# Weight sums of the second MLP: two sets kept in HBM against one, with the other grown in SBUF by adding transfers

## The chip, the cores and the metric

One core of a Trainium2 chip. The metric is the device time of one execution in microseconds; the time of a kernel is the median of several runs, and a lower one is better. A profile is taken of one further execution, and its times are counted from the first instruction of that execution.

## The reference, cut to what matters

A two-layer decoder trunk on 512 tokens of 1024 channels, all in float32. Layer 0 mixes tokens with a Mamba-2 SSD, layer 1 with HGRN2. After each mixer comes a layer norm, a squared-ReLU MLP, a second layer norm and a gate:

```
for i in range(2):
    mix = ssd_mixer(x, ...) if i == 0 else hgrn2_mixer(x, ...)
    h = layer_norm(ALPHA * x + mix)
    h = layer_norm(ALPHA * h + (relu(h @ w1[i]) ** 2) @ w2[i])     # w1: 1024 x 4096, w2: 4096 x 1024
    x = h + sigmoid(h @ w_gate[i]) * (p[i] @ w_proj[i])
```

"MLP 1" below is that of layer 0 and "MLP 2" that of layer 1.

## The kernel before, in words

**Three products for one.** Every float32 matrix product is made of three matmuls on a rounded high part and a low part of each operand (`mm3`, lines 121 to 123). A weight tile of 128 x 1024 values (512 KB) arrives by a DMA that the SyncE queue (SP) issues into a ring of three buffers called `raw` (`unit`, line 107). ScalarE (ACT) then rounds it into `whi` (line 114) and VectorE (DVE) subtracts to get `wlo` (line 117); there are six buffers of each. `split` does the same two steps for a tile that is already in SBUF. "The 512 KB unit" below means one such tile.

**Seven block products for eight.** Both MLPs replace a product of 2 x 2 blocks by seven products of sums of blocks, as Strassen and Winograd do. For that, sums of weight blocks are needed (t1 to t4 for w2; for w1 the four sums of `pair`) and sums of activation blocks (`half_blocks`: s1 to s4). The seven products are p1 (a11 with w00), p2 (a12 with w10), p6 (s2 with t2), p7 (s3 with t3), p5 (s1 with t1), p4 (a22 with t4), p3 (s4 with w11). Each is 24 matmuls of 512 columns and uses two weight units.

**The order within an MLP.** The 4096 hidden channels are worked in four groups. `hidden(g)` makes the activations of group g in steps "T"; `block_product` multiplies group g-1 with w2 in steps "Q" (or two "q"). `PERIODS` (MLP 1) and `PAIRS` (MLP 2) write out the order: period 0 has only T, periods 1 to 3 mix both, and period 4 is seven products back to back, with the layer norm of the first two token chunks (`after(0), after(1)`) before its last two products.

**The sums of w2 in MLP 1** are made by `weight_sums`: eight loads per group on the GpSimd (POOL) queue into `r` tiles (line 382), then DVE additions (lines 389 to 397), then `split`.

**The sums for MLP 2** are made in advance. `block_sums` is a generator of 64 steps; each step is one or two DMAs on the POOL queue that copy or add blocks from HBM to HBM (line 270): into `s1` for w1 and into `s2` for w2. `add_blocks` takes the next steps and makes each DMA depend on a recent instruction (`paced`). It is called after every Q of the periods 1 to 3 of MLP 1 (one step in period 1, two in 2 and 3: 7 + 14 + 14 = 35 steps), then during HGRN2 after two of three yields of `hcore` (the other 29). In MLP 2 `pair` loads the sums of w1 with `unit(both(..))`, and `block_product` gets `stored`, so that t1 to t4 are loaded from `s2` with `unit` as any weight. In the profile both tensors have the name `s`, all loads of MLP weights `in_w`.

**Other places with tiles held together.** `gate` code of layer 0 (`mlp_and_gate`, after the periods) holds one unit of `wp` and four of `wg` at a time, for each half of the output columns. `out_project` with a norm behind it holds four units, and the next MLP's first three tiles follow it. `last_gate` loads its own block sums into `tb` tiles on POOL (lines 461 to 468).

**Tile scheduler.** Apart from TensorE in some stages, the order on each engine is set at build time by priorities: `tc.high_priority(offset=...)` moves instructions ahead (`LEAD` 100, `SOON` 40, `SUMS` up to 300). Each engine's queue is then executed in that order.

Of the kernel before, what the change touches and what calls it, by code (L numbers as in the profile page):

```python
# [8 lines left out]
F32 = mybir.dt.float32  # L9
# [6 lines left out]
P = 128  # L16
# [29 lines left out]
def trunk(ctx: ExitStack, tc, a):  # L46
# [4 lines left out]
    whip = pool("whip", 6)  # L51
    wlop = pool("wlop", 6)
    b8 = pool("b8", 9)
# [22 lines left out]
    mlp = dict(r=8, blk=2, sg=2)  # L76
    bufs = dict(ssd=dict(two, xs=4, sz=4, y=2, xdt=2, ecs=2, ss=2), mlp0=mlp, hgrn=dict(two, xs=4, sz=4, cv=4, y=2, pv=2, btok=2, sc=2, scb=2, qd=2), mlp1=dict(tb=4, blk=2, sg=2))
    phase = []
# [46 lines left out]
    class Split:  # L125
# [9 lines left out]
        def l(self, k, sl=slice(0, T)):  # L135
            return self.lo[k // 4][:, k % 4, sl]

    def project(src, xs, ps, m=P, tok=slice(0, T)):
# [94 lines left out]
    def block_sums():  # L233

        w1, w2, s1, s2 = (a[n] for n in ("w1_1", "w2_1", "s1", "s2"))
        rows = lambda v: v.rearrange("u p n -> (u p) n")
        wv = w1.rearrange("(q i) p (h n) -> i h q p n", i=2, h=2)
        sv = s1.rearrange("q p s n -> s q p n")
        for g in range(4):
            wa, wb, wc, wd = (rows(w2[8 * g + 2 * i : 8 * g + 2 * i + 2]) for i in range(4))  # L240
            t1, t2, t3, t4 = (rows(s2[8 * g + 2 * i : 8 * g + 2 * i + 2]) for i in range(4))
# [33 lines left out]
    def transpose_split(src, dst, c, apart, keep=None, whole=None):  # L275

        sl = slice(c * P, (c + 1) * P)
        for q in range(2):
            pt = bank(psm, "pm") if (c == 3 if keep is not None else apart and q) else bank(pst, "pt")
            for j in range(4):  # L280
                k = 4 * q + j
                nc.tensor.transpose(pt[:, j * P : (j + 1) * P], src[:, k * P : (k + 1) * P], ident)
            v = pt.rearrange("p (j t) -> p j t", j=4)
            h = dst.hi[q][:, :, sl]
            with tc.high_priority(offset=LEAD if apart or keep is not None else SOON):
                nc.scalar.copy(h, v)
                turned_last[:] = [nc.vector.tensor_sub(dst.lo[q][:, :, sl], v, f32(h))]
# [43 lines left out]
    def norm(i, keep=None, whole=None):  # L331

        gb = ln_params(i)
        h_s = Split(8)
        sums = mk(sm, [P, NCH, 2], "lnsum") if i else None
# [10 lines left out]
    def half_blocks(blk, z0, z1, p, plus):  # L346
# [52 lines left out]

    def block_product(w, blk, lead, first, after=None, turns=None, sums=None, low=None, stored=None):  # L400

        if stored is None:
            t1, t2, t3, t4 = weight_sums(w, lead, after=low)
        else:
            t1, t2, t3, t4 = stored
        seen = set() if first else {(i, j) for i in range(2) for j in range(2)}
        banks = {}

        def product(x, f, name, start, i, j, turns=None):
            made = stored is None and any(f is t for t in (t1, t2, t3, t4))  # L410
            us = [split(v) if made else unit(v) for v in f]
            if start:
                banks[name] = [bank(psy, "py%d" % c) if name == "x" else bank(psj, "pj") for c in range(2)]
            t = blk[x]
            for c in range(2):
# [10 lines left out]
                with tc.high_priority(offset=SOON if after else 0):  # L426
                    minus = stored is not None and j == 1
                    if after and x in ("a12", "s1", "a22", "s4"):
# [19 lines left out]
        p3 = lambda: product("s4", w[1][1], "x", False, 0, 1, turns)  # L448
        for f in (p1, p7, p6, p4, p5, p2, p3) if after else (p1, p2, p6, p7, p5, p4, p3):
            yield from f()  # L450
            if after and f is p5:
                after(0), after(1)
# [4 lines left out]
    def last_gate(wp, wg, h_s, p_s, kept, turned):  # L457
# [12 lines left out]
        pairs = [mk(b8, [P, 2, 4, 256], "b8", F32R) for _ in range(2)]  # L470
        cells = [mk(b8, [P, 4, T], "b8") for _ in range(3)] + [tmp("blk", [P, 4, T])]
        cell = lambda n: cells[n // 4][:, n % 4, :]
        tok = lambda c: slice(c * P, (c + 1) * P)
# [35 lines left out]
        def final(c, h, g, pp, pin=None):  # L509
            sg = tmp("sg", [P, T])  # L510
            with behind(pin):
# [164 lines left out]
    def mlp_and_gate(layer, h_s, last, whole=None):  # L676
# [5 lines left out]
        def hidden(g):  # L682
            names = ("a11", "a12", "a22", "s1", "s2", "s3", "s4")
            blocks[g] = {
                n: tmp("blk", [P, 2, 4, 256], F32R) if n in ("s3", "s4") else mk(b8, [P, 2, 4, 256], "b8", F32R)
                for n in names
            }
            for p in range(2):
# [17 lines left out]
                for r in range(2):  # L706
                    z = mk(w4, [P, 2, T], "ab"[r])
                    for i in range(2):
# [15 lines left out]
        for g, period in enumerate(PAIRS if whole is not None else PERIODS):  # L724
            if g < 4:
                tiles = hidden(g)
            if g > 0:
                if g == 4:
# [8 lines left out]
                w = [[[w2[8 * g - 8 + 4 * i + 2 * j + u] for u in range(2)] for j in range(2)] for i in range(2)]  # L737
                stored = [[a["s2"][8 * g - 8 + 2 * i + u] for u in range(2)] for i in range(4)] if whole is not None else None
                products = block_product(
                    w, blocks.pop(g - 1), SUMS[g - 1], g == 1, *((after, turned(0), sums) if g == 4 else ()), low=low if g == 1 else None, stored=stored  # L740
                )
# [720 lines left out]
    with tc.manual_schedule(engines={mybir.EngineType.PE}):  # L1462
        for h in range(0, 8, 2):
# [141 lines left out]
```

## Time and profile before

| what | value |
|---|---|
| median of 3 runs | 1451.97 us (1451.65 to 1452.2) |
| the profiled execution's own time | 1448.33 us |
| its span, first to last instruction | 1446.6 us |
| TensorE (PE) busy | 1412.2 us (98%), granted clock 0.992 |
| DVE / ACT / POOL busy | 1082.4 / 806.1 / 104.7 us |
| moved by DMA queue q1 (issued by SP) | 166.24 MB |
| moved by DMA queue q0 (issued by POOL) | 88.09 MB |

The stages follow one another: SSD until about 372 us, MLP 1 and its gate until about 800, HGRN2 until about 1050, MLP 2 until about 1370, the last gate until the end. PE is the busiest engine by far, so a microsecond counts where PE waits, or where its matmuls run at a lower granted clock; the idle time of the others counts only through that. A DMA "lands" when its data are complete; the time from issue to landing is what a consumer sees. "DMA share" is the mean busy share of the 16 DMA engines.

### The profile page before, as it was taken

What the parts mean: (1) busy time and instruction counts of PE and PEld (TensorE: products, weight loads), DVE (VectorE), ACT (ScalarE), POOL (GpSimd) and SP (SyncE); (2) the same over time, 40 slices, a digit from 0 to 9 for tenths busy, and PEclk for the clock granted to TensorE, in tenths of its full rate; (3) what the DMA queues carried; (4) which work ended last, traced back from release to release, by engine and by line L of the source; (5) the groups of instructions that cost most, each with busy time, mean ns of one, the idle gap of its engine ahead of it and who ended that gap; (6) DMA issues with size and microseconds to landing.
All of it is one profiled execution on the core that took longest, in us unless ns stands there. A gap on an engine that the chain in (4) does not pass through costs nothing.

```text
span 1446.6 us, 21844 instructions
## 1 busy us (share of the span) xinstructions
PE 1412.2 (98%) x8505; PEld 1189.2 (82%) x8505; DVE 1082.4 (75%) x1824; ACT 806.1 (56%) x1252; POOL 104.7 (7%) x148
## 2 busy tenths in 40 slices
PE   9999999999999999998899999999999999999898
PEld 7888888888988888786677888888799988888677
DVE  7989587788967657657767756777788776866795
ACT  6766465562453543544354656665577556664573
POOL 0000000001002011121200002122100000000000
PEclk9999999999999999998999999999999999999999
DMA  8434333235336678999961337988875656568731
GB/s 304 143 105 137 96 104 115 87 113 194 103 102 186 193 207 278 230 280 251 277 235 63 100 104 169 237 244 223 209 220 190 188 169 198 167 194 243 245 110 58
DMA packets 68904, 255.72 MB, mean 177 GB/s; under 512 B 7489, under 2 KB 8257, under 8 KB 66369
## 3 DMA queue, kind: packets, MB, share of 16 engines
q1 hardware_dynamic: 47424, 166.24, 34.2%
q0 software_dynamic: 21376, 88.09, 24.3%
q8 instruction: 67, 1.10, 0.3%
q14 instruction: 37, 0.30, 0.1%
HBM read 251.09 MB, written 65.08 MB: 219 GB/s over the span
## 4 chain that ended last, share of the span: by engine, by line
PE 41%; DVE 5%; DMA 5%; ACT 2%; issue 1%; ACTq 0%; DVEq 0%; SPq 0%
PE pj L121 9%; PE pj L122 9%; PE pj L123 9%; PE py L121 2%; PE py L122 2%; PE py L123 2%; DVE wlo L117 2%; DMA raw<-s 2%; DMA raw<-in_w 1%; ACT whi L114 1%; DMA raw<-in_wg 1%; PE py L1310 1%; PE pt L121 1%; PE pm L121 1%; DMA raw<-in_wp 1%
## 5 line engine op out<-in xcount | busy, mean ns | idle before, releaser
L117 DVE TENSOR_TENSOR wlo<-raw,whi 128x1024 fp32r<-128x1024 f32 (+1 forms) x278 | 330.5, 1194 | 195.4 <-ACT whi L114 194.1
L114 ACT CAST whi<-raw 128x1024 fp32r<-128x1024 f32 (+1 forms) x278 | 285.2, 1028 | 319.6 <-PE pj L122 149.4
L121 PE MATMUL pj<-b,whi 128*128 128x512 f32 (+1 forms) x878 | 323.3, 369 | 3.1 <-DVE b L668 2.4
L122 PE MATMUL pj<-b,whi 128*128 128x512 f32 (+1 forms) x878 | 321.4, 366 | 0.0
L123 PE MATMUL pj<-b,wlo 128*128 128x512 f32 (+1 forms) x878 | 321.0, 366 | 0.0
L123 PE MATMUL pj<-whi,b 128*128 128x512 f32 x520 | 204.1, 393 | 0.0
L121 PE MATMUL pj<-whi,b 128*128 128x512 f32 x508 | 202.1, 398 | 0.0
L122 PE MATMUL pj<-wlo,b 128*128 128x512 f32 x508 | 199.6, 393 | 0.0
L121 PEld LDWEIGHTS pj<-b,whi 128*128 128x128 f32 x878 | 165.5, 189 | 29.9 <-DVE b L668 2.8
L122 PEld LDWEIGHTS pj<-b,whi 128*128 128x128 f32 x878 | 165.9, 189 | 26.5 <-issue 0.9
L123 PEld LDWEIGHTS pj<-b,wlo 128*128 128x128 f32 x878 | 165.7, 189 | 25.8
L123 PEld LDWEIGHTS pj<-whi,b 128*128 128x128 f32 x520 | 98.0, 188 | 20.2
L121 PEld LDWEIGHTS pj<-whi,b 128*128 128x128 f32 x508 | 95.5, 188 | 19.3 <-ACT b L1457 0.3
L122 PEld LDWEIGHTS pj<-wlo,b 128*128 128x128 f32 x508 | 95.5, 188 | 18.4 <-issue 0.2
L121 PE MATMUL py<-whi,b 128*128 128x512 f32 x248 | 98.7, 399 | 9.1 <-DVE acc L435 7.0
L123 PE MATMUL py<-whi,b 128*128 128x512 f32 x260 | 102.5, 395 | 0.0
L122 PE MATMUL py<-wlo,b 128*128 128x512 f32 x248 | 98.1, 396 | 1.3 <-DVE wlo L117 1.3
L270 POOL DMA_DIRECT2D s<-in_w x66 | 61.1, 986 | 335.9 <-issue 149.0
L114 ACT CAST whi<-r 128x1024 fp32r<-128x1024 f32 x40 | 41.6, 1051 | 43.7 <-PE pj L123 18.4
L121 PEld LDWEIGHTS py<-whi,b 128*128 128x128 f32 x248 | 47.4, 191 | 20.8 <-DVE acc L435 9.1
L117 DVE TENSOR_TENSOR wlo<-r,whi 128x1024 fp32r<-128x1024 f32 x40 | 48.1, 1217 | 14.2 <-ACT whi L114 14.2
L123 PEld LDWEIGHTS py<-whi,b 128*128 128x128 f32 x260 | 49.5, 190 | 10.4
(437 smaller groups left out, 2416.6 us busy)
## 6 DMA issues: line engine op xcount, KB each, us to landing
raw<-in_w SPq DMA_DIRECT2D x98, 512.0 KB, 4.4
raw<-s SPq DMA_DIRECT2D x60, 512.0 KB, 4.1
s<-in_w POOLq DMA_DIRECT2D x42, 512.0 KB, 7.6
raw<-in_wssd SPq DMA_DIRECT2D x36, 512.0 KB, 3.9
r<-in_w POOLq DMA_DIRECT2D x32, 512.0 KB, 8.8
s<-in_w POOLq DMA_DIRECT2D x16, 1024.0 KB, 11.9
a<-csd SPq DMA_DIRECT2D x16, 512.0 KB, 3.7
raw<-in_wso SPq DMA_DIRECT2D x16, 512.0 KB, 3.3
```

The lines of the kernel that those rows point to most:

```text
L114: nc.scalar.copy(hi[:, :n], f)
L117: nc.vector.tensor_sub(lo[:, :n], f, f32(hi[:, :n]))
L121: nc.tensor.matmul(out, sh, mh, start=start, stop=False, **kw)
L122: nc.tensor.matmul(out, sh, ml, start=False, stop=False, **kw)
L123: return nc.tensor.matmul(out, sl, mh, start=False, stop=stop, **kw)
L270: dma = nc.gpsimd.dma_start(out, src, **(dict(accum_op=ALU.add, max_dma_last_dim=8192) if add else {}))
L1310: nc.tensor.matmul(pcs[r][bs, at : at + n], kk[r][:, ts], qs, start=True, stop=True)
```

## The change

The sums of w2 for MLP 2 are no longer made in HBM: the tensor `s2` and its 32 steps go, and `block_sums` keeps the 32 steps for w1. After a Q of MLP 1 one step is taken, in the periods 1 and 2 only (14 steps); in HGRN2 one is taken after every second yield (24 places for the other 18).

In MLP 2 `block_product` gets `grown`. Two pairs of `r` tiles are filled on the POOL queue: t3 = w11 and then + w01; t1 = w01 and then + w00. When t3 has been split for p7, w00 is added to the same tiles, which makes t2; when that has been split for p6, w10 is added, which makes t4. Each is a DMA with an add into SBUF. The order of the products becomes p1, p2, p7, p6, p4, p5, p3 (last group: p1, p7, p6, p5, p4, p2, p3).

Buffers: `wlo` has five buffers, not six; the `r` ring of this stage has four; the activation block s3 moves to the pool `b8`; the input of MLP 2 is held in four `b8` tiles cut by token halves (`Blocks`); the fourth of the first four tiles is projected in two halves of 256 tokens; the last gate's `sg` and one spare tile come from the `r` ring.

```diff
-    wlop = pool("wlop", 6)
+    wlop = pool("wlop", 5)
...
-    bufs = dict(..., mlp1=dict(tb=4, blk=2, sg=2))
+    bufs = dict(..., mlp1=dict(tb=4, r=4))
...
+    class Blocks:
+        def __init__(self):
+            self.t = [[mk(b8, [P, 2, 4, 256], "b8", F32R) for _ in range(2)] for _ in range(2)]
...
     def block_sums():        # the eight steps per group that write s2 are removed
-            yield [(t1, wb, False)]
             yield small(o2, b11, True)
-            yield [(t3, wb, False)]
             yield small(o4, o2, False)
-            yield [(t1, wa, True)]
             yield small(o4, b12, True)
-            yield [(t3, wd, True)]
-            yield [(t2, t3, False)]
-            yield [(t2, wa, True)]
-            yield [(t4, t2, False)]
-            yield [(t4, wc, True)]
...
-        put("s2", a11)
-        put("s3", a21)
+        put("s3" if plus else "s2", a21 if plus else a11)
+        put("s2" if plus else "s3", a11 if plus else a21)
...
-    def block_product(w, blk, lead, first, after=None, turns=None, sums=None, low=None, stored=None):
-        if stored is None:
+    def block_product(w, blk, lead, first, after=None, turns=None, sums=None, low=None, grown=False):
+        if grown:
+            t2, t1 = ([tmp("r", [P, 1024]) for _ in range(2)] for _ in range(2))
+            t3 = t4 = t2
+            def add_to(t, v, start=False):
+                for u in range(2):
+                    nc.gpsimd.dma_start(t[u], v[u], **({} if start else dict(accum_op=ALU.add)))
+            with tc.high_priority(offset=lead):
+                add_to(t3, w[1][1], True)
+                add_to(t1, w[0][1], True)
+                add_to(t3, w[0][1])
+                add_to(t1, w[0][0])
+            grow = {"s3": w[0][0], "s2": w[1][0]}
+        else:
             t1, t2, t3, t4 = weight_sums(w, lead, after=low)
-        else:
-            t1, t2, t3, t4 = stored
+            grow = {}
...
         def product(x, f, name, start, i, j, turns=None):
-            made = stored is None and any(f is t for t in (t1, t2, t3, t4))
-            us = [split(v) if made else unit(v) for v in f]
+            us = [split(v) if any(f is t for t in (t1, t2, t3, t4)) else unit(v) for v in f]
+            if x in grow:
+                with tc.high_priority(offset=LEAD):
+                    add_to(t2, grow[x])
...
+        if grown:
+            order = (p1, p7, p6, p5, p4, p2, p3) if after else (p1, p2, p7, p6, p4, p5, p3)
...
-        cells = [mk(b8, [P, 4, T], "b8") for _ in range(3)] + [tmp("blk", [P, 4, T])]
+        cells = [mk(b8, [P, 4, T], "b8") for _ in range(3)]
+        spare = tmp("r", [P, T])
...
-                            project(unit(w1[tiles[2 * r + i]], after=low if g == 0 and r == 0 else None), h_s, ps)
+                            u = unit(w1[tiles[2 * r + i]], after=low if g == 0 and r == 0 else None)
+                            for tok in [slice(0, T)] if whole is None else [slice(0, 256), slice(256, T)]:
+                                project(u, h_s, ps, tok=tok)
...
-                if op == "Q" and not last and g < 4:
-                    add_blocks(2 if g > 1 else 1)
+                if op == "Q" and not last and g in (1, 2):
+                    add_blocks()
...
-                if at % 3:
+                if at % 2:
                     add_blocks()
...
-    args["s2"] = nc.dram_tensor("s2", (32, P, D), F32).ap()
```

More of the change, by code (lines that the diff above doesn't have):

```diff
@@ L233, in block_sums @@
     def block_sums():
-        w1, w2, s1, s2 = (a[n] for n in ("w1_1", "w2_1", "s1", "s2"))
-        rows = lambda v: v.rearrange("u p n -> (u p) n")
+        w1, s1 = a["w1_1"], a["s1"]
         wv = w1.rearrange("(q i) p (h n) -> i h q p n", i=2, h=2)
@@ L426, in product @@
                 with tc.high_priority(offset=SOON if after else 0):
-                    minus = stored is not None and j == 1
+                    minus = grown and j == 1
                     if after and x in ("a12", "s1", "a22", "s4"):
@@ L448, in block_product @@
         p3 = lambda: product("s4", w[1][1], "x", False, 0, 1, turns)
-        for f in (p1, p7, p6, p4, p5, p2, p3) if after else (p1, p2, p6, p7, p5, p4, p3):
+        if grown:
+            order = (p1, p7, p6, p5, p4, p2, p3) if after else (p1, p2, p7, p6, p4, p5, p3)
+        else:
+            order = (p1, p7, p6, p4, p5, p2, p3) if after else (p1, p2, p6, p7, p5, p4, p3)
+        for f in order:
             yield from f()
-            if after and f is p5:
+            if after and f is order[4]:
                 after(0), after(1)
@@ L684, in hidden @@
             blocks[g] = {
-                n: tmp("blk", [P, 2, 4, 256], F32R) if n in ("s3", "s4") else mk(b8, [P, 2, 4, 256], "b8", F32R)
+                n: tmp("blk", [P, 2, 4, 256], F32R) if n == "s4" or n == "s3" and whole is None else mk(b8, [P, 2, 4, 256], "b8", F32R)
                 for n in names
@@ L737, in mlp_and_gate @@
                 w = [[[w2[8 * g - 8 + 4 * i + 2 * j + u] for u in range(2)] for j in range(2)] for i in range(2)]
-                stored = [[a["s2"][8 * g - 8 + 2 * i + u] for u in range(2)] for i in range(4)] if whole is not None else None
                 products = block_product(
-                    w, blocks.pop(g - 1), SUMS[g - 1], g == 1, *((after, turned(0), sums) if g == 4 else ()), low=low if g == 1 else None, stored=stored
+                    w, blocks.pop(g - 1), SUMS[g - 1], g == 1, *((after, turned(0), sums) if g == 4 else ()), low=low if g == 1 else None, grown=whole is not None
                 )
```

25 lines of the change are left out of this document (17 added, 8 removed).

## The prediction

> **What bounds the kernel now.** I read the cores' view first, then busy time by stage (columns: window, its length, then PE, PEld, DVE, ACT, POOL busy with their counts, the granted clock, the DMA share and GB/s).
>
> ```profile
> core 0: 1446.6 us, clock 0.992
> 372.00:592.00 220.00, 220.00 (x1039) 184.96 (x1039) 153.39 (x179) 104.49 (x135) 25.72 (x37) 1.00 0.63 189
> 592.00:730.00 138.00, 122.28 (x512) 98.49 (x511) 95.05 (x126) 62.31 (x85) 30.37 (x42) 0.94 0.95 262
> 785.00:800.00 15.00, 11.75 (x49) 9.13 (x48) 11.35 (x14) 5.99 (x11) 0.00 (x0) 0.89 0.17 55
> 850.00:1010.00 160.00, 160.00 (x1761) 131.51 (x1760) 118.78 (x377) 96.06 (x222) 27.75 (x33) 1.00 0.79 205
> 1010.00:1065.00 55.00, 53.28 (x405) 44.90 (x404) 42.53 (x87) 33.85 (x87) 7.51 (x10) 1.00 0.89 231
> 1065.00:1320.00 255.00, 254.37 (x1667) 231.95 (x1666) 195.32 (x255) 166.56 (x248) 1.34 (x2) 1.00 0.58 184
> 1320.00:1362.00 42.00, 35.55 (x161) 28.24 (x160) 27.68 (x35) 18.31 (x23) 5.25 (x8) 0.96 0.87 252
> ```
>
> PE is full wherever the DMA share is up to 0.79, and loses time in three places with a share of 0.87 or more: 138.00 - 122.28 = 15.72 us at the end of MLP 1, 42.00 - 35.55 = 6.45 us at the end of MLP 2, 1.72 us at the end of HGRN2. Only these, and 3.25 us in the gate at 785, can be won. The timeline of PE names the first place's waits, in brackets:
>
> ```profile
> 594.44 0.50 PE L121 MATMUL py<-whi,b 128*128 128x512 f32 x1 [1.40 <-DVE acc L435]
> 668.29 0.80 PE L121 MATMUL py<-whi,b 128*128 128x512 f32 x1 [2.82 <-DVE acc L435]
> 675.79 1.22 PE L121 MATMUL pj<-whi,blk 128*128 128x512 f32 x2 [2.99 <-ACT whi L114]
> 686.31 0.50 PE L122 MATMUL py<-wlo,b 128*128 128x512 f32 x1 [1.28 <-DVE wlo L117]
> 718.88 1.11 PE L282 MATMUL pt<-cst,acc 128*128 128x128 f32 x4 [5.95 <-DVE acc L225]
> 728.47 0.66 PE L282 MATMUL pt<-cst,acc 128*128 128x128 f32 x4 [1.18 <-DVE b L287]
> ...
> 597.32 0.39 PE L121 MATMUL pj<-b,whi 128*128 128x512 f32 x1
> 597.54 0.39 PE L122 MATMUL pj<-b,whi 128*128 128x512 f32 x1
> ...
> 668.89 0.63 PE L122 MATMUL py<-wlo,b 128*128 128x512 f32 x1
> 669.32 0.63 PE L123 MATMUL py<-whi,b 128*128 128x512 f32 x1
> ...
> 721.50 0.63 PE L123 MATMUL pj<-whi,b 128*128 128x512 f32 x1
> 721.93 0.63 PE L121 MATMUL pj<-whi,a 128*128 128x512 f32 x1
> ```
>
> Matmuls normally start 0.227 us apart; after the three long waits they start 0.43 us apart, 6 + 9 + 6 = 21 of them from 668.89 to 721.93: the clock was halved. That is another 21 x 0.2 = 4.2 us.
>
> The releasers are DVE and ACT, but what do these wait for? The ACT timeline, the chain of waits, the DMA views of two windows (a quiet one, 400 to 460, then 592 to 730; last column: us to landing), and POOL's timeline:
>
> ```profile
> 706.45 1.05 ACT L114 CAST whi<-raw 128x1024 fp32r<-128x1024 f32 x1 [5.56 <-DMA raw<-in_wp]
> 715.79 9.63 DMA raw<-in_wp
> ...
> raw<-in_w SPq DMA_DIRECT2D x8, 512.0 KB, 3.3
> r<-in_w POOLq DMA_DIRECT2D x6, 512.0 KB, 3.7
> ...
> q0 software_dynamic: 5841, 24.13, 69.0%
> s<-in_w POOLq DMA_DIRECT2D x13, 512.0 KB, 8.1
> raw<-in_w SPq DMA_DIRECT2D x12, 512.0 KB, 7.2
> r<-in_w POOLq DMA_DIRECT2D x8, 512.0 KB, 12.5
> raw<-in_wg SPq DMA_DIRECT2D x7, 512.0 KB, 9.6
> 722.72 0.87 POOL L270 DMA_DIRECT2D s<-in_w  x1 [7.52 <-DMA s<-s]
> ```
>
> POOL's queue fills 69% of the DMA engines, mostly with the sums for MLP 2, whose last transfer here leaves at 722.72. Beside it a 512 KB load takes 7 to 10 us, not 3.3. With three `raw` buffers and ACT and DVE in fixed order, the late load holds up everything behind its cast: layer norm and evictions included.
>
> **The change, part by part.**
>
> *Fewer steps in MLP 1.* Of 35 steps 14 stay, all in periods 1 and 2. One step lands in about 8.1 us, 14 x 8.1 = 113 us; two periods of 8 T and 7 Q last 2 x 15 x 24 x 0.227 = 163 us. So nothing is left over for period 3 and the seven products behind it: after about 590 only MLP 1's own loads run, as in 400 to 460. Waits that I take as gone: the two on `acc` (1.40 and 2.82; ACT was late with a cast before the burst of `half_blocks`), both layer norm waits (5.95 and 1.18; the loads of 706.45 and 715.79 stand ahead of them). With them 12 slow matmuls: 1.40 + 2.82 + 5.95 + 1.18 + 12 x 0.2 = 13.7 us. I leave standing the 2.99 and 1.28, since DVE makes the last group's sums only after p1's eviction, an order that fast loads need not mend. Bounds: all 15.72 + 4.2 = 19.9 gone, or only the two layer norm waits and six slow matmuls, 8.3.
>
> *HGRN2.* 18 steps for 29, and over before the last norm. PE is full in 850 to 1010, so nothing is gained there; of the 1.72 us after it I take half, -0.8 (0 to -1.7). The gate's 3.25 us at 785 have a DMA share of 0.17, so no load causes them: 0 (up to -3.25 if DVE's order changes).
>
> *Sums grown in MLP 2.* Per group, SP loads lose 8 units (stored sums); POOL gains 12 transfers, 4 starts and 8 adds. ACT and DVE do the same casts and subtractions. The rows of the end of MLP 2 (chain, DMA view of 1320 to 1362, POOL's timeline, groups; behind a queue stand its packets, MB and share):
>
> ```profile
> 1335.65 6.22 DMA raw<-s
> 1346.57 6.59 DMA raw<-s
> q1 hardware_dynamic: 1757, 6.39, 44.4%
> q0 software_dynamic: 1144, 4.18, 42.6%
> tb<-in_wg POOLq DMA_DIRECT2D x6, 512.0 KB, 6.7
> 1356.22 0.86 POOL L468 DMA_DIRECT2D tb<-in_wg  x1 [7.74 <-DMA tb<-tb]
> ...
> L117 DVE TENSOR_TENSOR wlo<-raw,whi 128x1024 fp32r<-128x1024 f32 (+1 forms) x278 | 330.5, 1194 | 195.4 <-ACT whi L114 194.1
> L114 ACT CAST whi<-raw 128x1024 fp32r<-128x1024 f32 (+1 forms) x278 | 285.2, 1028 | 319.6 <-PE pj L122 149.4
> ...
> 1050.88 0.28 PE L121 MATMUL pj<-b,whi 128*128 128x256 f32 x1
> 1051.00 0.28 PE L122 MATMUL pj<-b,whi 128*128 128x256 f32 x1
> ```
>
> Now the last seven products need 14 units in 7 x 5.45 us through three buffers, each held for 6.2 + 1.0 + 1.2 = 8.4 us: too slow. After the change 8 of the 14 bypass `raw`, so most of the 6.45 us goes; I count 5. In its place comes a chain: t3 split, add issued (0.86), landed (6.7), cast (1.03), subtracted (1.19) = 9.8 us, with p7 (5.45 us) to cover it. If the split ends when p7 starts, PE waits 4.35 us; if one product earlier, nothing. I take 3, since tiles for two products fit in five `wlo` buffers only just. From p6 to p4 there are two products (10.9 us), so nothing, unless POOL stands behind a `tb` wait (7.74 us, as above), which would cost 9.8 + 7.74 - 10.9 = 6.6. Sum -2, bounds -6.45 and +11. In the middle groups T steps lie between the products: a T is about 28 matmuls of 0.12 us = 3.4 us, so p7's start to p6's start is 5.45 + 2 x 3.4 = 12.2 us: hidden at a landing of 6.7.
>
> DMA load: per byte POOL's adds cost more (4.18 MB in 0.426 x 42 us: 234 GB/s) than SP's loads (6.39 MB in 18.6 us: 343). Per group 4.2 MB at 343 go (12 us), 6.3 MB at 234 come (27 us): +15 in 80 us, a share of 0.58 + 0.18 = 0.76, below the 0.79 at which PE was full. And fewer loads share the `raw` ring.
>
> The Trainium skill, "DMA: Bandwidth & Descriptors", section "Anatomy of one DMA — SWDGE (gpsimd) path", fits a transfer from GpSimd as 2.0 us + bytes/436e3, an estimate of 3.2 us here. The quiet row of 3.7 nearly agrees, the adding row of 6.7 does not; by it the chain would be 6.3 us, its stall under 1, and the forecast 2 us lower.
>
> *Five `wlo` tiles, all stages.* No row shows a wait for a `wlo` buffer; the nearest is the 1.19 us of one subtraction. Costs can arise where five units are held at once (the gate: one of `wp`, four of `wg`, so four subtractions come late, 4.8) and before two norms (1.2). I take 1.5, bounds 0 and 6. PE works 5.45 us on a unit in the other stages, so they hide it.
>
> *Fourth tile in halves.* 48 x 0.12 - 24 x 0.227 = +0.3 us. *s3 in `b8`, token blocks, order of products, `sg` from `r`:* same instructions; a buffer of the norm's output comes free after the first four tiles, ahead of the first `half_blocks`: 0.
>
> Sum: -13.7 - 0.8 - 2 + 1.5 + 0.3 = -14.7. The profiled execution took 1448.33 us (span 1446.6), so 1433.6; the median of the runs shown stands 3.64 higher, 1451.97, so **1437**.
>
> The Trainium skill, "TensorE: Matmul & The Clock Gate", Part 1, has half rate after at least one idle window of about 3.4 us. The row of 668.29 shows it after 2.82 us. By the page the shorter waits would cost no clock, and the forecast would be about 1 us higher.
>
> **The rivals.**
>
> *A, the adds arrive too late (slower).* Place: p6 and p4 of every group of MLP 2. It begins where landing exceeds 6.7 + (12.2 - 9.8) = 9.1 us. For it: 12.5 us for `r<-in_w` at a share of 0.95. Against: the 0.76 above. At 12.5: 3.4 us x 2 x 3 groups = 20, with the last group's 11 against -12.7 from the rest: 1452 + 18 = 1470; it turns the sign from about 10.5 us.
>
> *B, DVE's fixed order and not the transfers.* DVE is busy 95 of 138 us in 592 to 730 and several waits sit behind its bursts. Then only the layer norm goes, 8.3 for 13.7: 1443.
>
> *C, the fifth buffer binds,* at its bound of 6: 1442.
>
> *D, everything goes:* 19.9 + 3.25 + 1.7 + 6.45 = 31, 1421.
>
> *E, the transfers only shift* and a backlog still reaches 700: no gain, 1451. Against: 113 us in 163.
>
> **How the numbers follow.** A difference under 0.2% (2.9 us) cannot be told from none. Forecast 0.52 (its own range 1430 to 1443), B 0.15, C 0.08, D 0.08, E 0.06, A 0.11. Leaving out D and A, 1424 to 1454 holds 0.81. Faster: forecast, B, C, D less a little for the upper tail, 0.81; same: E and a little, 0.07; slower: A, 0.12.
>
> **What would show it.** Right: DMA share in 592 to 730 near 0.4, loads of `in_wg` at about 4 us, no PE wait on `acc` L225 above 2 us; the gap at 675 about 3 us still there; one wait of 3 us before p6 in the last group of MLP 2. Wrong: PE waits on `whi` or `wlo` made from `r` in the middle groups (A); the 592 to 730 waits unchanged at a low share (B); waits on `wlo` in the gate (C).

## The result, and the profile after

The changed kernel takes 1469.8 us (median; 1467.99 to 1475.22), the kernel before on the same chip 1451.8 us: a ratio of 1.0134, 95% interval [1.0104, 1.0163]. It is slower by 18 us; the forecast was 1437 us. The profiled execution took 1467.99 us. Its cores' view and busy time by stage (columns as before the change):

```profile
core 0: 1466.2 us, clock 0.988
592.00:730.00 138.00, 131.43 (x583) 107.28 (x582) 114.73 (x151) 71.43 (x99) 11.66 (x19) 0.99 0.55 176
850.00:1010.00 160.00, 158.16 (x1784) 130.18 (x1772) 118.41 (x362) 98.46 (x246) 28.77 (x31) 1.00 0.76 179
1065.00:1320.00 255.00, 243.38 (x1573) 220.22 (x1572) 184.45 (x243) 156.17 (x233) 23.50 (x31) 0.99 0.68 191
1320.00:1380.00 60.00, 39.70 (x188) 32.56 (x186) 29.56 (x37) 22.28 (x30) 12.73 (x17) 0.83 0.87 221
```

The end of MLP 1 has gained as foreseen: 131.43 of 138 us where there were 122.28, at a DMA share of 0.55 for 0.95. What was full before is full no longer: 11.6 us are idle in the middle of MLP 2, where 0.6 were, and 20.3 of 60 at its end. I cut the run at PE's transposes of the layer norms (the row at 718.88 of before, the one at 708.11 of after, and so on) and at the last transposes of the gate, to get lengths of stages that can be compared from kernel to kernel, in us of the profiled execution:

| stage | before | after |
|---|---|---|
| MLP 1 up to its norm | 340.0 | 327.9 |
| gate of layer 0 | 76.1 | 69.1 |
| HGRN2 | 243.5 | 247.2 |
| norm between HGRN2 and MLP 2 | 22.6 | 28.0 |
| MLP 2 up to its norm | 322.9 | 351.6 |

That is -19.1 in the first two and +37.8 in the last three; the spans differ by 19.6. The waits of PE in after (us in total, times, longest):

```profile
PE pj L121 <- ACT b L363: 17.1, 1, 17.1
PE py L121 <- DVE acc L460: 9.4, 4, 4.9
PE pj L121 <- ACT a L683: 8.0, 3, 4.6
PE pt L292 <- ACT b L301: 3.7, 1, 3.7
PE pt L292 <- DVE acc L246: 1.9, 2, 1.7
```

One wait of 17.1 us stands out. It lies in the last group of MLP 2; the timelines of PE, then ACT, then POOL around it:

```profile
1369.51 0.80 PE L121 MATMUL pj<-whi,b 128*128 128x512 f32 x1 [17.07 <-ACT b L363]
1370.11 0.63 PE L122 MATMUL pj<-wlo,b 128*128 128x512 f32 x1
1370.53 0.63 PE L121 MATMUL pj<-whi,b 128*128 128x512 f32 x1
...
1341.84 1.99 ACT L114 CAST whi<-r 128x1024 fp32r<-128x1024 f32 x2
1363.27 1.04 ACT L114 CAST whi<-r 128x1024 fp32r<-128x1024 f32 x1 [16.37 <-DMA r<-in_w]
1367.90 1.04 ACT L114 CAST whi<-r 128x1024 fp32r<-128x1024 f32 x1 [3.07 <-DMA r<-in_w]
1368.85 1.14 ACT L363 CAST b<-a 128x512 fp32r<-128x512 f32 x2
...
1343.84 0.84 POOL L493 DMA_DIRECT2D tb<-in_wg  x1 [2.10 <-DMA tb<-in_wg]
1350.39 0.56 POOL L494 DMA_DIRECT2D tb<-tb  x1 [5.71 <-DMA tb<-in_wg]
1355.43 0.85 POOL L495 DMA_DIRECT2D tb<-in_wg  x1 [4.48 <-DMA tb<-tb]
1355.97 1.18 POOL L418 DMA_DIRECT2D r<-in_w  x1
1361.30 0.56 POOL L496 DMA_DIRECT2D tb<-tb  x1 [4.15 <-DMA tb<-in_wg]
1361.84 0.92 POOL L418 DMA_DIRECT2D r<-in_w  x1
```

Read from the bottom. The tiles of t3 are cast at 1341.84 and VectorE's subtractions of them end at 1344.3 and 1346.1, so the adds that turn them into t2 (`r<-in_w`, L418) could leave then; they left at 1355.97 and 1361.84. They stand in POOL's queue behind the last gate's `tb` transfers, each of which waits for the one before: 5.71 and 4.48 us for the first add, 4.15 more for the second. ACT, which has the casts of t2 next in its order, stands 16.37 us, and behind it stand the half-block casts (L363) that PE needs for the product before. PE resumes at half rate, 0.43 us from matmul to matmul.

The second finding is in VectorE's waits, before and then after:

```profile
DVE wlo L117 <- ACT whi L114: 208.3, 126, 6.7
```

```profile
DVE wlo L117 <- PE pj L123: 59.9, 36, 4.4
DVE wlo L117 <- ACT whi L114: 55.3, 27, 15.9
DVE wlo L117 <- issue: 20.3, 17, 3.8
```

Before, a low part waited for its high part and for nothing else. After, it waits 36 times for PE's last pass with the oldest `wlo` tile, 59.9 us in all.

### The profile page after: what moved, and what is told of

It reads as the page before. It is cut to its first block, busy times and chain, and to the rows that moved or that the text cites. A ratio compares the mean times of both kernels' runs of the same rounds, so it can differ in the third digit from the quotient of the medians.

```text
span 1466.2 us, 21904 instructions
## 1 busy us (share of the span) xinstructions
PE 1412.5 (96%) x8529; PEld 1189.9 (81%) x8529; DVE 1085.6 (74%) x1824; ACT 807.2 (55%) x1252; POOL 118.3 (8%) x164
## 4 chain that ended last, share of the span: by engine, by line
PE 73%; DMA 10%; issue 7%; DVE 7%; ACT 3%; POOL 1%; DVEq 0%; POOLq 0%; ACTq 0%; SPq 0%
PE pj L121 18%; PE pj L122 18%; PE pj L123 18%; DMA r<-in_w 4%; PE py L121 3%; PE py L123 3%; PE py L122 3%; DMA raw<-in_w 2%; DVE wlo L117 2%; ACT whi L114 1%; PE py L1072 1%; DMA tb<-in_wg 1%; PE pt L292 1%; DMA raw<-s 1%; PE py L1341 1%
## 5 line engine op out<-in xcount | busy, mean ns | idle before, releaser
L114 ACT CAST whi<-raw 128x1024 fp32r<-128x1024 f32 x246 | 252.1, 1026 | 314.9 <-PE pj L122 137.2
L117 DVE TENSOR_TENSOR wlo<-raw,whi 128x1024 fp32r<-128x1024 f32 x246 | 291.8, 1192 | 126.4 <-PE pj L123 43.6
L121 PE MATMUL pj<-whi,b 128*128 128x512 f32 x540 | 215.5, 399 | 17.3 <-ACT b L363 17.1
L123 PE MATMUL pj<-whi,b 128*128 128x512 f32 x552 | 216.7, 393 | 0.0
L122 PE MATMUL pj<-wlo,b 128*128 128x512 f32 x540 | 212.7, 394 | 0.0
L121 PEld LDWEIGHTS pj<-whi,b 128*128 128x128 f32 x540 | 102.0, 189 | 38.5 <-ACT b L363 17.5
L117 DVE TENSOR_TENSOR wlo<-r,whi 128x1024 fp32r<-128x1024 f32 x72 | 87.9, 1223 | 46.6 <-ACT whi L114 18.2
L123 PEld LDWEIGHTS pj<-whi,b 128*128 128x128 f32 x552 | 103.8, 188 | 21.2
L122 PEld LDWEIGHTS pj<-wlo,b 128*128 128x128 f32 x540 | 102.0, 189 | 20.0 <-DVE wlo L117 0.4
L114 ACT CAST whi<-r 128x1024 fp32r<-128x1024 f32 x72 | 74.9, 1050 | 72.4 <-DMA r<-in_w 35.4
L121 PEld LDWEIGHTS py<-whi,b 128*128 128x128 f32 x248 | 47.6, 192 | 21.5 <-DVE acc L460 6.2
L392 POOL DMA_DIRECT2D r<-in_w x32 | 18.6, 584 | 524.8 <-DVE acc L316 336.1
L418 POOL DMA_DIRECT2D r<-in_w x48 | 37.1, 822 | 277.4 <-ACT b L690 124.7
```

The costliest lines, as they stand in the source:

```text
L114: nc.scalar.copy(hi[:, :n], f)
L117: nc.vector.tensor_sub(lo[:, :n], f, f32(hi[:, :n]))
L121: nc.tensor.matmul(out, sh, mh, start=start, stop=False, **kw)
L122: nc.tensor.matmul(out, sh, ml, start=False, stop=False, **kw)
L123: return nc.tensor.matmul(out, sl, mh, start=False, stop=stop, **kw)
L392: queue.dma_start(t[i][u], src)
```

## The experiments

Two theories to start with: **L1**, the fifth `wlo` buffer costs far more than its bound, because a late subtraction keeps its `raw` buffer and so makes the next load late; **Q**, the grown sums themselves are harmless and only their place in the queues of the last group costs. The rival to both is that growing by adding transfers is too slow anywhere. Ratios are to the kernel before, on the same chip as the run. Experiments 1 to 4 ran on one chip, 5 to 8, 9 to 12, and 13 and 14 on three others, and the kernel before took 1447.3, 1452.3, 1451.2 and 1452.4 us there. So times in us from two of these groups can be compared only to about 5 us; for such pairs the difference of the ratios is given too.

**1 and 2: the part of the change outside MLP 2, with six and with five low tiles.** Edit of the kernel before: the 32 steps for `s2` removed, the pacing of the changed kernel, and MLP 2 reading plain tiles of w2 in the stored form, so that it leaves the sums of w2 out; then the same with one line more.

```diff
-                stored = [[a["s2"][8 * g - 8 + 2 * i + u] ...
+                stored = [[w2[8 * g - 8 + 2 * i + u] ...
-                if op == "Q" and not last and g < 4:
-                    add_blocks(2 if g > 1 else 1)
+                if op == "Q" and not last and g in (1, 2):
+                    add_blocks()
-                if at % 3:
+                if at % 2:
(second kernel only)
-    wlop = pool("wlop", 6)
+    wlop = pool("wlop", 5)
```

> The kernel before with the changed pacing and without the 32 steps for w2; MLP 2 keeps its old form, six low tiles and loads through the raw ring, but loads plain tiles of w2 in place of their sums (the sums of w2 in MLP 2 are left out). It has the gain of MLP 1 alone. Theory 'the gain is real and MLP 2 gives it back': 1434 to 1441 us, DMA share in 592 to 730 near 0.5, MLP 2 as long as before. Rival 'the gain at the end of MLP 1 is only shifted into the gate or HGRN2': 1448 to 1453 us.

> The run before it with five low tiles and nothing else changed (same computation left out). Theory L 'the fifth low tile holds raw buffers back and makes loads late': 6 to 14 us over the one with six, with VectorE's subtraction waiting for TensorE (a buffer to come free), which it never does with six. Rival 'five are enough': within 2 us of it.

Measured: 1418.4 us (0.9796 [0.9777, 0.9815]) with six and 1437.1 us (0.9917 [0.9886, 0.9948]) with five. The first is 16 us better than the range that I expected, so the gain outside MLP 2 is larger than forecast; in the second the fifth buffer costs 18.7 us, more than the 6 to 14 expected. The end of MLP 1 and VectorE's waits with six, and then with five:

```profile
592.00:730.00 138.00, 137.90 (x627) 113.59 (x626) 114.00 (x149) 71.61 (x100) 9.77 (x17) 1.00 0.50 163
DVE wlo L117 <- ACT whi L114: 158.8, 114, 4.2
DVE wlo L117 <- PE pj L123: 2.2, 1, 2.2
```

```profile
592.00:730.00 138.00, 133.43 (x602) 109.05 (x601) 115.34 (x151) 70.25 (x98) 11.16 (x19) 1.00 0.50 169
DVE wlo L117 <- PE pj L123: 63.8, 37, 4.4
```

With six, PE is full at the end of MLP 1, at the same DMA share. MLP 1 and gate are 317.5 and 70.4 us long with six, 324.2 and 68.9 with five; HGRN2 242.6 against 246.3, MLP 2 322.2 against 329.5.

**3: the gate's transfers behind the last adds on POOL.** The changed kernel with:

```diff
-        with tc.high_priority(offset=SOON):
+        with tc.high_priority(offset=SOON), behind(last_add[0]):
             nc.gpsimd.dma_start(t3, wg[4])
```

> The changed kernel with the last gate's tb transfers queued on GpSimd behind the last group's adds; nothing else. Theory Q 'the 17 us stall before p7 of the last group is the add for t2 standing behind tb transfers in GpSimd's queue (1344 to 1356)': the stall falls from 17 to about 6 us, 1457 to 1461 us. Rival 'the add's own landing sets it': 1467 to 1472 us.

**4: ScalarE's casts of t2 behind the half-block casts**, likewise in the last group only:

```diff
+            with behind(last_put[0] if grown and after and x == "s2" else None):
-            us = [split(v) ...
+                us = [split(v) ...
```

> The changed kernel with ScalarE's two casts of t2 in the last group queued behind the casts of half_blocks; nothing else. Theory O 'p7 waits only because ScalarE stands at the cast of t2 ahead of the casts that p7 needs': p7 runs, p6 then waits for t2; 17 us become about 11, 1462 to 1466 us. If the transfer does not matter once the order is right: 1453 us. Rival 'order plays no part': 1467 to 1472 us.

**6: both together.**

> The changed kernel with both: tb transfers behind the adds on GpSimd and the casts of t2 in the last group behind those of half_blocks. Theories Q and O together leave only the add's own chain: no wait over 3 us in the last group, 1439 to 1445 us, that is 2 to 8 us over the stored form with five low tiles (1437). If the adds cost more than that elsewhere in MLP 2: about 1450 us.

Measured: 1447.3 us (1.0002 [0.9974, 1.0031]), 1458.6 (1.0076 [1.0046, 1.0107]) and 1456.6 (1.003 [1.0007, 1.0052]). POOL's order alone is worth 22 us (19 by the ratios), ScalarE's alone 11 (8), where I had expected 9 to 13 and 4 to 8; MLP 2 shrinks from 351.6 to 331.9 and 349.1. Together they bring no more than the first alone; I had expected 1439 to 1445, and why it is not so I cannot say. The 9 us between the medians of 3 and 6 carry little: 5 of them lie between the two chips, and the two kernels scatter by 17 and 13 us from run to run (1439.1 to 1456.0 and 1450.4 to 1463.1). Both stay slower than the stored form with five low tiles, by 10 us (3) and by about 16 us going by the ratios (6). So with five low tiles something else in the grown form costs too; the growing of t1 in `r` is in both kernels, and no run took it out with five low tiles, so its price stays open. PE's longest wait in each of the three, in this order:

```profile
PE pj L121 <- ACT b L364: 6.3, 1, 6.3
```

```profile
PE py L121 <- ACT whi L114: 8.0, 2, 7.3
```

```profile
PE pt L294 <- DVE acc L246: 6.7, 2, 6.3
```

The 17.1 us are gone from each. In the second the wait has moved on to the tile itself: with ScalarE free, PE reaches p6 before t2 is there.

**5: five low tiles and four raw ones,** the second kernel with `RAWS = 4`: does the cost of the low ring come through the raw ring?

> The thinned kernel with stored form and five low tiles (sums of w2 in MLP 2 left out), with four raw buffers in place of three. Theory L1 'with five low tiles a raw buffer waits for its subtraction, so the next load starts late': the fourth raw buffer gives most of the loss back, 1420 to 1428 us. Rival L2 'VectorE itself stands at a subtraction that has no buffer, and what is queued behind it is late': 1433 to 1439 us, VectorE's waits for TensorE as with three.

Measured: 1421.2 us (0.9782 [0.9753, 0.9812]). A line of VectorE's waits:

```profile
DVE wlo L117 <- PE pj L123: 55.7, 36, 4.4
```

VectorE still stands 36 times for PE, as with three raw buffers, and 16 of the 18.7 us are back, all of them by the ratios (0.9782 against 0.9796 with six). So the late subtraction costs next to nothing by itself; what costs is the raw buffer that it holds, whose next load starts late. That is L1.

**9: the kernel before with five low tiles,** one line changed.

> The kernel before with five low-part tiles instead of six and nothing else changed. Theory L1 (with five low tiles the low-part subtraction waits for a matmul that is done with the oldest of them, the raw buffer is held until then, and the next load on SyncE's queue starts late): the price is that of the pair of stored-form kernels with six and five (1418.4 to 1437.1, so 18.7) or a little more, because the transfers of this kernel's first MLP are slower: +15 to +25, 1462 to 1475, with VectorE's waits for TensorE ahead of the low-part subtraction, 50 us or more of them, which the kernel before does not have. Rival: the fifth buffer costs only where the loads are quick and the tensor engine is the bound at every tile; here the transfers bound the end of the first MLP anyway, and the time is within 5 us of the kernel before.

Measured: 1471.1 us (1.0139 [1.0112, 1.0166]), that is +19.9: as slow as the changed kernel, by one character. Its waits of VectorE:

```profile
DVE wlo L117 <- PE pj L123: 72.2, 41, 4.4
```

MLP 1 and gate lose only 2.1 us here (341.8 and 76.4), as the rival says of a stage that transfers bound anyway; HGRN2 (253.1), the norm (29.8) and MLP 2 (329.3) lose 9.6, 7.2 and 6.4 in the profiled execution, which ran a little over the median (span 1473.2).

**10: six low tiles, five high ones.** The first kernel with `whip` 5.

> The thin stored form (32 block-sum steps, stored sums' tiles replaced by plain tiles of w2, so sums of w2 are left out) with six low-part tiles and five high-part tiles. If what costs is that a raw buffer is held until both of its halves have a free tile (theory L1), it is the same whichever ring is short: a cast then waits for a matmul, 1430 to 1442, like the five low tiles (1437.1). The high part is made first and is used by two of the three matmul passes, so its tile is free about as late as the low part's. Rival: only the low ring binds, since the subtraction comes last of the three steps: 1416 to 1422.

Measured: 1428.5 us (0.9843 [0.9823, 0.9864]), between the two expectations, so neither held. A short high ring costs 10 us (7 by the ratios) and a short low ring 18.7. Why it costs about half or less was not tried.

**7: everything at once.** Experiment 6 with six low tiles; to make room `r` has three buffers, the spare tile leaves that ring, and t1 is summed in the raw ring (a load on SP, an adding transfer on POOL).

```diff
+    def summed_unit(src, more, lead=LEAD):
+        with tc.high_priority(offset=lead):
+            raw = mk(raws, [P, 1024], "raw")
+            nc.sync.dma_start(raw, src)
+            nc.gpsimd.dma_start(raw, more, accum_op=ALU.add)
+        return split(raw, lead)
```

> The changed kernel with six low tiles: t1 is summed in the raw ring (load by SP, add by GpSimd into the raw tile), so three r tiles do; the order on GpSimd and ScalarE as in the run before it. Everything is computed. If the fifth low tile and the order of the last group were all that was wrong: 1420 to 1428 us. If growing in place costs by itself: 1432 to 1442 us.

Measured: 1448.2 us (0.9981 [0.996, 1.0001]), 20 us over what I expected. PE's waits, and ACT and POOL around one of them:

```profile
PE pj L128 <- ACT b L695: 24.7, 4, 8.6
...
1132.58 1.04 ACT L121 CAST whi<-raw 128x1024 fp32r<-128x1024 f32 x1 [9.79 <-DMA raw<-in_w]
...
1122.07 0.84 POOL L428 DMA_DIRECT2D r<-in_w  x1 [5.27 <-DMA r<-in_w]
1125.26 0.86 POOL L114 DMA_DIRECT2D raw<-in_w  x1 [2.35 <-DMA raw<-in_w]
```

The row at 1122.07 is the add that makes the next group's t3, which waits for its own start. The add for t1 stands behind it on POOL, and then still 2.35 us for its own load, so here the load ends its wait last. The raw tile is held meanwhile, for a load and then for an add, and the cast behind it waits 9.79 us. Up to MLP 2 the run is that of experiment 1 (MLP 1 317.5, HGRN2 242.6); MLP 2 takes 348.6. So I had lengthened the hold on a raw buffer once more, by another way.

**11 and 13: one pair of grown tiles only.** The same without t1's add (t1 is a plain tile of w2, so w00 is left out of it); t3, t2 and t4 still grow. In 13 the two queue orders of the last group are put back as the change has them.

```diff
-                    us = [summed_unit(w[0][1][u], w[0][0][u]) for u in range(2)]
+                    us = [unit(w[0][1][u]) for u in range(2)]
```

> The changed kernel with six low-part tiles, three raw buffers, the turned-over POOL and ScalarE orders of the last group, and the sum t1 of MLP 2 replaced by a plain tile of w2 (so w00 is left out of t1); t2, t3, t4 still grow in place by adding transfers. It lacks the raw add of the run with six low tiles (1448.2), whose three new waits of 7.2 to 8.6 us stood on that add. If growing in place costs next to nothing once its queue is in order, 1420 to 1428 (the thin stored form ran at 1418.4). If growing itself loses time in the middle groups (their waits of 2 to 5 us in the changed kernel), 1432 or more.

> The kernel of the run with two grown sums (1418.8; six low-part tiles, three raw buffers, t1 of MLP 2 a plain tile of w2, so w00 is left out of t1) with the two queue orders of the last group as the changed kernel has them: the gate's `tb` transfers ahead of the group's last adds on POOL, the casts of t2 ahead of those that p7 needs on ScalarE. If the wait of 17 us in the last group stands on those orders, whatever the depth of the low ring, it is back: 1430 to 1440, with one PE wait of 8 to 17 us at L128 for ScalarE's half-block cast. Rival: with six low tiles and without t1's adds in POOL's queue the gate's transfers are through in time, and the time stays at 1417 to 1423.

Measured: 1418.8 us (0.978 [0.9758, 0.9802]) and 1428.2 (0.9832 [0.9796, 0.9868]). The first equals the stored form's 1418.4: with queues in order and six low tiles, growing t3, t2 and t4 costs nothing that can be measured, though MLP 2 is 1.4 us longer. The halves of the fourth tile, the token blocks and the order of the products are in it too, so they cost nothing that can be measured either. The second shows the last group's fault with six low tiles, 9.3 us (7.5 by the ratios; MLP 2 takes 332.7 us against 323.6), 2 us short of the range that I expected. The wait is of the size expected, but PE stands for an eviction (`acc`) behind VectorE's subtraction and not for a half-block cast. Experiment 11 has this wait too, with 5.17 us, so only the rest of it stands on the queue orders. PE, ACT, and POOL of 13:

```profile
1337.35 0.76 PE L128 MATMUL py<-whi,b 128*128 128x512 f32 x1 [8.94 <-DVE acc L472]
...
1330.02 1.04 ACT L121 CAST whi<-r 128x1024 fp32r<-128x1024 f32 x1 [10.49 <-DMA r<-in_w]
...
1317.22 0.86 POOL L507 DMA_DIRECT2D tb<-in_wg  x1 [4.39 <-DMA tb<-tb]
1323.44 0.56 POOL L508 DMA_DIRECT2D tb<-tb  x1 [5.37 <-PE py L130]
1324.05 1.73 POOL L428 DMA_DIRECT2D r<-in_w  x2
```

Again the adds leave directly after the `tb` row that waited.

**8 and 12: the kernel before, only paced otherwise.** All 64 steps and both tensors stay. In 8, 21 steps go into periods 1 and 2, none into period 3, 8 into the gate's second half, 8 into HGRN2's projections (the text before run 12 says 4; the code has 8); in 12, 28 into periods 1 and 2, 4 into the gate, none into the projections.

```diff
-                if op == "Q" and not last and g < 4:
-                    add_blocks(2 if g > 1 else 1)
+                if op == "Q" and not last and g in (1, 2):
+                    add_blocks(g)                      # 12: add_blocks(2)
...
-                nc.vector.tensor_add(d, sg, d)
+                paced[0] = nc.vector.tensor_add(d, sg, d)
+                if h == 1:
+                    add_blocks(2)                      # 12: add_blocks()
...
+                if h < 2 and k in (2, 6):              # in the projections; not in 12
+                    add_blocks()
```

> The kernel before, all 64 steps and both tensors in HBM, six low tiles, only issued elsewhere: 7 and 14 steps in periods 1 and 2 of MLP 1, none in period 3, 8 in the second half of the gate, 8 in the first units of HGRN2, the rest in HGRN2 as before. Theory 'only the transfers beside the end of MLP 1 hurt': 1424 to 1434 us. Rival 'the same transfers cost as much beside the gate and HGRN2': 1444 to 1452 us.

> The kernel before with all 64 block-sum steps for both tensors of MLP 2 and six low-part tiles, only issued at other places: two per pair of tiles in groups 1 and 2 of the first MLP (28), none at its end, one per chunk of the gate's second half (4), and the other 32 in HGRN2 at the places it had. The run with 21 steps in those groups, 8 in the gate and 4 in the HGRN2 projections took 1433.6 and lost 13 us in HGRN2 against the kernel before. If that loss is the number of steps packed into HGRN2 and its projections, it goes back to 2 to 4 and the time is 1420 to 1428. Rival: the steps moved into groups 1 and 2 bring the first MLP's waits back there (transfers of the block sums beside the loads), and the time stays at 1432 to 1440.

Measured: 1433.6 us (0.9873 [0.9847, 0.9898]) and 1447.0 (0.9983 [0.9963, 1.0003]). In 8, MLP 1 is 318.6 us long, as short as with half the steps, but HGRN2 takes 256.4. In 12 HGRN2 takes 245.0, as expected, but MLP 1 333.6 and the norm 30.0: the rival was right in kind, though the time is 7 us above its range. The end of MLP 1 and a stretch of HGRN2 in 8, then the end of MLP 1 in 12 and a row of its POOL:

```profile
592.00:730.00 138.00, 137.30 (x624) 112.99 (x623) 117.37 (x153) 73.18 (x102) 13.21 (x21) 1.00 0.61 191
850.00:1010.00 160.00, 156.73 (x1735) 129.31 (x1734) 114.98 (x350) 98.66 (x244) 31.32 (x36) 1.00 0.90 233
```

```profile
592.00:730.00 138.00, 130.06 (x562) 105.30 (x561) 108.89 (x140) 63.98 (x88) 20.09 (x29) 0.96 0.73 216
...
642.03 2.03 POOL L270 DMA_DIRECT2D s<-in_w  x2 [8.84 <-issue]
```

The table of before has PE full up to a share of 0.79 and short of it from 0.87 on. Here 0.61 is full, and 0.90 in HGRN2 is not. Of the 28.9 us that experiment 1 gained with half the steps, 18.8 are to be had by moving all 64. In 12, at 0.73, PE loses time under that bound, and so do the 0.68 and 0.76 of after: a share averaged over 138 us doesn't show when the transfers come. The row of POOL says when they come in 12: the steps of periods 1 and 2 run late, and the last of them leave at 642, where in 1 and 8 they leave at 600 and 616. PE's waits of 2.82 and 2.99 us at the end of MLP 1 are back, at 666 and 674. That is the backlog of rival E. Whether fewer than seven extra steps in period 1 would do was not tried.

**14: t1 stored, t2 to t4 grown.** Experiment 11 with t1 made in HBM as before the change: 8 steps more, 40 in all, four of them at the gate.

```diff
+            yield [(t1, wb, False)]
             yield small(o2, b11, True)
             yield small(o4, o2, False)
+            yield [(t1, wa, True)]
...
-                    us = [unit(w[0][1][u]) for u in range(2)]
+                    us = [unit(t1_stored[u]) for u in range(2)]
```

> The whole computation: the run with two grown sums (1418.8) with t1 of MLP 2 stored in HBM like the first weights' sums (8 more block-sum steps, 40 in all, four of them at the gate's second half and two more of the rest in HGRN2), six low-part tiles, three raw buffers, both queue orders of the last group. If the steps' number only costs where they crowd (the run with 64 of them re-paced lost 0 to 13 us in HGRN2), 8 more cost at most 3: 1418 to 1424, ahead of the fastest complete kernel so far (1433.6). If every block-sum step costs about what the two runs with 64 show (1433.6 and 1447.0 against 1418.4 for 32: 0.5 to 0.9 us a step), 1422 to 1426.

Measured: 1424.5 us (0.9805 [0.9778, 0.9833]): inside the second range and half a us above the first, so it does not tell the two apart. It is some 45 us below the changed kernel and 28 below the one before: the best here that computes everything. MLP 1, gate and HGRN2 are 317.5, 70.3 and 242.6, MLP 2 327.4. Its end of MLP 1 and its waits of VectorE:

```profile
592.00:730.00 138.00, 137.99 (x628) 113.67 (x626) 113.13 (x149) 70.76 (x98) 9.74 (x17) 1.00 0.50 158
DVE wlo L124 <- ACT whi L121: 166.9, 110, 4.7
```

## Why the prediction was wrong, point by point

**Fewer steps in MLP 1 (forecast -13.7): right in kind, too small.** The loads that bounded the end of MLP 1 landed nearly as forecast; the DMA view of after, 592 to 730:

```profile
raw<-in_w SPq DMA_DIRECT2D x13, 512.0 KB, 4.3
r<-in_w POOLq DMA_DIRECT2D x8, 512.0 KB, 4.1
raw<-in_wg SPq DMA_DIRECT2D x7, 512.0 KB, 3.4
```

The last block sums of after leave at 609 us, not at about 590 as counted. Both layer norm waits went. With six low tiles MLP 1 gained 22.5 us and the gate 5.7 (experiment 1). I had left 2.99 and 1.28 us standing as an order of VectorE, and put the gate at 0; they went too: from 560 to 780 the view lists no PE wait any more. That is more than rival D's 19.9 and 3.25. In after itself 12.1 and 7.0 are left, since the fifth buffer takes some back; of that a PE wait of 4.9 us at 599 is the visible part.

**HGRN2 (forecast -0.8):** -0.9 with six low tiles; +3.7 in after, where PE is busy 158.16 of the 160 us in which it was full. Experiment 2, with five, has 246.3 us, so nearly all of it is the fifth buffer.

**Five low tiles (forecast +1.5, bounds 0 to 6): the first step that failed.** Measured +18.7 and +19.9 in two kernels. I priced the delay of a subtraction, 1.19 us or four of them, and hid it behind PE's 5.45 us for a unit. What a buffer costs is not how late the instruction is that waits for it, but what that instruction holds meanwhile: here one of three raw buffers, and with it a load of 3 to 4 us on the queue of SP. "No row shows a wait for a `wlo` buffer" was true and said only that six were enough. The places named, gate and norms, were also wrong: the waits are spread over the run, 36 of them on `pj`.

**Grown sums at the end of MLP 2 (forecast -2): the second step that failed.** The mechanism was named, "unless POOL stands behind a `tb` wait", priced at +6.6, and then counted at 0. Three such waits came, 5.71, 4.48 and 4.15 us, since the `tb` transfers are a chain in which each waits for the last. And I followed only who waits for the add, p6, not what is queued behind the waiting cast on ScalarE: the half blocks of the product before. Together 17.1 us and a slowed clock; POOL's order was worth 19 to 22 us with five low tiles and both orders 7.5 to 9.3 with six, so the fault costs more beside a short low ring.

The term that I did count shows where the queues are in order, in experiment 11. Before's waits in the last 64 us of MLP 2, 8.0 us of idle PE together, are gone, as forecast (-5). In their place stands one wait ahead of p6, with half rate behind it:

```profile
1334.76 0.80 PE L128 MATMUL py<-whi,b 128*128 128x512 f32 x1 [5.17 <-DVE acc L472]
```

It is the chain of add, cast and subtraction: the cast of t2's second tile waited 3.3 us for its add, and the eviction that PE needs is queued behind it. I had taken 3 us for its stall, out of 0 to 4.35. So the -2 came out near 0: MLP 2 in experiment 11 is 0.7 us longer than before the change.

**Middle groups (forecast 0):** three waits of 8.0 us together, released by ScalarE. The longest stands behind the cast of a `raw` tile that landed late, not of an `r` tile:

```profile
1177.79 0.58 PE L121 MATMUL pj<-tb,whi 128*128 128x256 f32 x1 [4.64 <-ACT a L683]
1176.42 1.04 ACT L114 CAST whi<-raw 128x1024 fp32r<-128x1024 f32 x1 [3.12 <-DMA raw<-in_w]
```

Only the shortest, 0.68 us, follows a wait for an `r` tile. ScalarE did wait for those tiles, in after from 1065 to 1372:

```profile
ACT whi L114 <- DMA r<-in_w: 35.4, 10, 16.4
```

Of the 35.4 us 16.37 and 3.07 are the last group's, shown above; PE stood for little of the rest. How much of the 8.0 us is the fifth buffer and how much the growing was not separated.

**The rivals.** A's 1470 is the time that was measured, by another way: it asked for landings over 9.1 us at p6 and p4 of every group, and they took 5.7, starts and adds together, at a DMA share of 0.68 for the 0.76 forecast; the two late adds of the last group took about 7 and 6 us from issue to cast. The DMA view of after, 1065 to 1320:

```profile
r<-in_w POOLq DMA_DIRECT2D x31, 512.0 KB, 5.7
```

C named the buffer that mattered most, with a third of its price. B and E fell for the change: the waits at the end of MLP 1 went with the transfers. D's total of 1421 was about met by experiments 1, 11 and 14 (1418.4, 1418.8, 1424.5), but from other places: MLP 1 and the gate gave more than D has there, and MLP 2 gave nothing of D's 6.45.

Of the signs of a right forecast, loads of `in_wg` at 3.4 us and no wait above 2 us on the norm's `acc` came; the DMA share was 0.55 and not 0.4, and the gap at 675 shrank to 1.3 us. They watched only the half of the change that gained. The sign for the other half, a wait of 3 us before p6, came as 17.1 us before p7. The signs named for A and C, PE waits on `whi` or `wlo`, did not come (the middle groups have one, of 0.4 us): PE stood for evictions, copies and half blocks queued behind such tiles.

**The price of one transfer.** The Trainium skill, "DMA: Bandwidth & Descriptors", section "Anatomy of one DMA — SWDGE (gpsimd) path", gives an estimate of 3.2 us for a transfer of this size. In after the plain loads into `r` took 4.1 us (592 to 730, DMA share 0.55) and the starts and adds together 5.7, so the measured rows of 3.7 and 6.7 stood nearer; either price would have missed the three waits ahead of the adds.

## What to carry to other kernels

Rings that feed one another are one ring: before taking a buffer from the last of them, ask which instruction will stand for it and what that instruction still holds further up, and price the load that then starts late. Before a transfer that something needs goes onto a queue in fixed order, list what will stand ahead of it there and what each of these waits for, and behind the consumer's wait list what else its engine owes to PE. When a stage is freed and the total does not fall, run the freed stage with each resource that was given up restored: one line (six low tiles) told more here than any timeline. And compare times in us only on one chip, or as ratios to a common kernel.

## What the runs showed that I had not expected

- Kernels whose PE waits often scatter: 1430.3 to 1443.3 (experiment 2) and 1439.1 to 1456.0 (3), against 1417.3 to 1418.8 (1). It is not the five low tiles alone: the kernel before, with six, took 1443.0 to 1453.3 in 15 runs on the same chip.
- A fourth raw buffer replaces a sixth low tile as far as can be measured (ratios of 0.9782 and 0.9796), though VectorE waits 55.7 us for PE in the one.
- A step of the block sums costs by where it stands: 32 more of them cost 11 to 15 us in experiment 8, nearly all of it in HGRN2, and 27 to 29 in 12, against experiment 1.
- Moving 64 steps to other places, with no other change, brought 19 us (experiment 8).
- Half rate does not set in at once after a wait: after the 3.23 us that PE stood until 1345.07 in after, the next five starts were 0.22 to 0.31 us apart, and only then 0.43. After 2.68 us, at 1262.67, none slowed down, and after the 2.82 us at 668.29 of before they did at once. So the clock's price cannot be read from the length of a wait alone.
